# Retention values of a hybrid decoder block in one 512-column unit behind attention

## The chip, the cores and the metric

The kernel runs on one core of a Trainium2 chip. The metric is device time in microseconds (us) of one launch; smaller is better. A core has five engines that work side by side and hand tiles to one another: TensorE (PE, matrix products), VectorE (DVE), ScalarE (ACT), GpSimd (POOL) and SyncE (SP, which here only starts transfers).

## The reference

One decoder block over 512 tokens of width 1024. Two branches stand side by side, a retention branch (4 heads, key width 128, value width 256) and a block-sparse attention (8 heads of 64). Each goes through an output projection, sigmoid gates mix them, and a SwiGLU block of hidden width 2816 follows.

```python
def reference(x, norm1_w, w_in, q_norm_w, k_norm_w, w_ret_out, w_moba_out, w_o,
              norm2_w, w_ffn_gate, w_ffn_up, w_ffn_down):
...
        h = rmsnorm(x, norm1_w[l])
        proj = h @ w_in[l]
        rq, rk, rv, rg, mq, mk, mv, ga, gb = jnp.split(proj, split_points, axis=-1)

        rq = rotary(rq.reshape(B, S, RET_HEADS, RET_DK), pos)
        rk = rotary(rk.reshape(B, S, RET_HEADS, RET_DK), pos) * (RET_DK ** -0.5)
        rv = rv.reshape(B, S, RET_HEADS, RET_DV)
        ret = jax.nn.silu(rg) * retention(rq, rk, rv)
        a = ret @ w_ret_out[l]
...
        b = moba_attention(mq, mk, mv) @ w_moba_out[l]

        mix = jax.nn.sigmoid(ga) * a + jax.nn.sigmoid(gb) * b
        x = x + mix @ w_o[l]

        h2 = rmsnorm(x, norm2_w[l])
        f = (jax.nn.silu(h2 @ w_ffn_gate[l]) * (h2 @ w_ffn_up[l])) @ w_ffn_down[l]
        x = x + f
```

Inside `retention`, for each head: scores of queries with keys times a decay mask, times the values, then a normalisation of each token over the head's 256 columns (mean and variance). The values `rv` are 1024 columns of the projection, 256 for each head. This change is about how they are computed and when.

## The kernel before

**Tiling.** A tile is 128 partitions by up to 512 columns of float32 (a full PSUM bank) or 1024 columns (SBUF). Each float32 operand is split in a high part, rounded to the format of TensorE (`fp32r`), and a low part, the rest; `mm3` (L470) makes one product out of three matmuls: high by high, high by low, low by high. The high part is a cast by ScalarE (L418 for weights: `wh<-raw`), the low part a subtraction by VectorE (`wl<-raw,wh`). VectorE and TensorE record through one helper, so their lines all read L222.

**Units.** The projections run as units of Strassen-Winograd: the inner width 1024 and the columns are halved, and seven products (B11, T1, T2, B21, B22, T3, T4) stand for eight. A product is 24 matmuls (8 pieces by `mm3`), a unit 168. Some of the weight operands are sums of weight quarters, made by the transfer itself (GpSimd's accumulating queue) or by VectorE (`raw<-raw,raw`). Results of the products are combined by ScalarE copies and VectorE adds when they leave PSUM. A unit of kind W has the weights stationary and 256 tokens moving; one of kind X has the activations stationary and the weights moving, 256 columns at a time (class `Quarters`) or 512 (class `WideQuarters`, two banks for each product).

**Order.** `ORDER` (L45) lists the units of the first half of the kernel: `rk` queries and keys of two retention heads, `rv` values of two heads (kind X, 256 columns), `rg` the retention gate, `ga` and `gb` the mixing gates, `b` and `a` the output projections of attention and of retention. `NORMAL` (L80) is the order of products in a unit; in it the bank of B21 is seeded by a ScalarE copy of B11's result, and `/` puts T4 off into the next unit. The weights follow the same plan: `load_w` starts the transfer of a weight tile as soon as an earlier one's buffer is free, `more_raws` adds or takes buffers.

**Work beside.** After every group of matmuls the kernel calls `advance` (which takes a step of the queue `later`: splits, rotary steps, copies out of PSUM) and `run_bg`, which takes one entry of the list `bg`: attention first, then retention. For each pair of heads, `rv_out` (L1265) splits the values and then queues `ret_scores` (L1293), `ret_values` (L1319), the gates and, after the last pair, `ret_finish` (L1378): statistics, `ret_norm`, and `ret_transpose`, which turns the normalised rows into `ret`, the moving operand of unit `a`. Everything runs in the order in which it is written on each engine; what stands between two engines is a semaphore wait.

**Ends.** In the SwiGLU block `Hidden.c11` (L1672) adds and applies Silu. `last` (L1757) writes the last rows out: one half copied by ScalarE and sent from its queue, the other copied by VectorE and sent from SyncE's.

Of the kernel before, what the change touches and what calls it, by code (L numbers as in the profile page):

```python
# [13 lines left out]
ALU = mybir.AluOpType  # L14
# [27 lines left out]
WIDE = 4  # L42
OEXTRA = 5
FEXTRA = -2
ORDER = (("rk", 0), ("rv", 0), ("gb", 0), ("rk", 1), ("rv", 1), ("rg", 1), ("gb", 1), ("b", 0), ("b", 1), ("ga", 0), ("a", 0), ("ga", 1), ("a", 1))  # L45
# [14 lines left out]
NLAG = 2  # L60
OAHEAD = (6, 10)
# [21 lines left out]
DOWN = "B11 B21 T1 T2 B22 T3 / T4"  # L83
ALONE = "B11 B21 T1 T2 B22 T3 T4z"


def weight_plan():
# [31 lines left out]
    for name, i in ORDER:  # L119
        if name == "rg":  # L120
            cols(C_RG + 512 * i)
        elif name == "rv":
            cols(C_RV + 512 * i)
        elif name == "rk":
            wino("w_in", C_RQ + 256 * i, "w_in", C_RK + 256 * i)
        elif name == "a":
            feat(sum([group("w_ret_out", (4 * i + ct) * P, KT) for ct in range(4)], []))
        elif name == "b":
            feat(sum([group("w_moba_out", (4 * i + ct) * P, 4) for ct in range(4)], []))
        else:  # L130
            c = {"ga": C_GA, "gb": C_GB}[name] + 512 * i
            wino("w_in", c + 256, "w_in", c)
# [37 lines left out]
def hybrid_block(ctx: ExitStack, tc: tile.TileContext, wall, xin, xtok, n2, cin, out):  # L170
# [652 lines left out]
    def wino_unit(w, ev, hooks={}):  # L823
# [22 lines left out]
        seed = order[1] != "B21"  # L846
# [79 lines left out]
    class WideQuarters:  # L926


        def __init__(self, out):
            self.out = out  # L930
            self.tiles = big(nm("qa")), big(nm("qb"))
            self.a, self.b = ((t[:, :512], t[:, 512:]) for t in self.tiles)

        def p1(self, x, i, z):
            A.copy(z[i], x[i])
# [7 lines left out]
        def c11(self, z, i):  # L943
            self.out(0, 0, i, z[i])
# [278 lines left out]
    def rot_out(h0):  # L1223
        def f(r, c, x):
# [32 lines left out]
            later(d + 4, lambda: V.tensor_tensor(part["L"], two(a), part["H"].bitcast(F32), ALU.subtract))  # L1257
        return f
# [6 lines left out]
    def rv_out(h0):  # L1265
        def f(pair, i, x):
            rv[h0 + i, pair] = split(f"rv{h0 + i}_{pair}", x, None, 0 if i == 0 else SLAG[1])
            if (pair, i) == (1, 0):
                a, b = ([lambda h=h, j=j: ret_scores(h, j) for j in range(NT)] for h in (h0, h0 + 1))
                v, w = ([lambda h=h, p=p: ret_values(h, p) for p in range(2)] for h in (h0, h0 + 1))  # L1270
                fs = gates(h0 // 2)
                bg.extend(a + fs[:3] + v + b + [fs[3], None, None] + w + [None])
                ret_done("rv")
        return f
# [17 lines left out]
    def ret_scores(h, j):  # L1292
# [15 lines left out]
        def first():  # L1308
            V.scalar_tensor_tensor(tmp, ps[:, d0:d0 + P], s, tri, ALU.mult, ALU.mult)
            if rest:  # L1310
                A.activation(H[:, o], ps[:, d0 + P:w], AF.Copy, scale=s)

# [9 lines left out]
    def ret_values(h, pair):  # L1322
        ps = side_ps()
        for i in (2 * pair, 2 * pair + 1):
            c = (i % 2) * 256
            for j in range(i + 1):
# [3 lines left out]
                    rv[h, j // 2][:, (j % 2) * 256:(j % 2) * 256 + 256], j == 0, j == i)  # L1330
        def stats():
            for i in (0, 1):
# [3 lines left out]
            if pair == 0:  # L1336
                ro[h, 0], ro[h, 1] = halves(f"ro{h}")
            A.copy(ro[h, pair], ps)
# [53 lines left out]

    def rv_unit(n):
        wino_unit(hW, Quarters(rv_out(2 * n)))
# [77 lines left out]
    def branch(cts, n, mov, evac):  # L1472
# [5 lines left out]
        "rg": rg_unit, "rk": rk_unit, "rv": rv_unit,  # L1478
# [9 lines left out]
    for name, n in ORDER:  # L1488
        make[name](n)
    assert not bg  # L1490
# [163 lines left out]
    class Hidden:  # L1654
# [17 lines left out]
        def c11(self, z):  # L1672
            if not self.whole:
                V.tensor_tensor(self.a0, z, self.a0, ALU.add)
                z = self.a0
# [79 lines left out]
    def last(banks, i):  # L1755
# [7 lines left out]
        for c, copy, queue in ((slice(0, 256), A.copy, nc.scalar), (slice(256, 512), V.tensor_copy, nc.sync)):  # L1763
            y = act(nm("y"))[:, :256]
            copy(y, banks[i][:, c])
# [89 lines left out]
```

## Time and profile before

| | us |
|---|---|
| median of 3 runs | 778.69 |
| lowest and highest of them | 778.56, 778.98 |
| the profiled execution, own time | 778.98 |
| span of its profile | 777.2 |

The span is the time from the first to the last record of the trace; the execution's own time has 1.8 us more around it. The profile gives the busy time of each engine, the chain of work that ended last, and for each instruction its start, its duration and what the engine waited for ahead of it. On TensorE, matmuls are pipelined: one lasts longer than the distance from its start to the next one's, so the pace is read from starts.

### The profile page before, as it was taken

The numbers are of one execution on the slowest core, as the hardware profiler recorded it, in microseconds if no ns is written. First come the engines' busy times: TensorE is split into PE (matmuls) and PEld (weight loads), VectorE is DVE, ScalarE is ACT, GpSimd is POOL, SyncE is SP. The second block draws the span as 40 slices with busy tenths as digits, with TensorE's granted clock in tenths as the row PEclk, the third lists the DMA queues.
The fourth block names the chain that finished last, engine by engine and source line by source line (L and its number), as shares of the span: only waits on it lengthen the run. The fifth ranks groups of instructions, "written<-read, shape, count | busy, mean of one in ns | idle before, by whom it ended". The sixth has DMA issues, their size and how long they took to land.

```text
span 777.2 us, 13314 instructions
## 1 busy us (share of the span) xinstructions
PE 770.4 (99%) x5224; PEld 702.1 (90%) x5224; DVE 630.8 (81%) x959; ACT 454.3 (58%) x746; POOL 68.7 (9%) x83
## 2 busy tenths in 40 slices
PE   9999999999999999999999999999999999999997
PEld 6888888889999998989988899989999899988996
DVE  7988688887797677758588998899787977789786
ACT  8656587876675485734355775655554455655451
POOL 0001000000101000000001000111001110110000
PEclk9999999999999999999999999999999999999999
DMA  9947542536768474554898714789556993779502
GB/s 327 356 121 191 129 83 65 140 102 158 190 169 203 115 216 112 163 136 132 256 330 243 177 36 115 195 196 292 159 149 153 266 263 103 171 209 288 119 2 109
DMA packets 40959, 134.85 MB, mean 174 GB/s; under 512 B 4544, under 2 KB 5568, under 8 KB 40896
## 3 DMA queue, kind: packets, MB, share of 16 engines
q1 hardware_dynamic: 29088, 94.41, 34.3%
q0 software_dynamic: 11376, 39.06, 28.5%
q8 instruction: 41, 0.67, 0.4%
q10 hardware_dynamic: 432, 0.52, 0.2%
q14 instruction: 22, 0.18, 0.1%
HBM read 131.88 MB, written 2.10 MB: 172 GB/s over the span
## 4 chain that ended last, share of the span: by engine, by line
PE 86%; DVE 5%; issue 3%; ACT 3%; DMA 2%; POOL 0%; SPq 0%; ACTq 0%; DVEq 0%; POOLq 0%
PE pm L222 78%; PE ps L222 8%; DMA raw<-wall 2%; DVE wl L222 1%; DVE h L222 1%; DVE ws L222 1%; ACT wh L418 1%; DVE mx L222 1%; ACT f L1594 0%; ACT p L1115 0%; DVE qb L222 0%; DVE rot L222 0%; POOL raw L345 0%; ACT h L1582 0%; DVE gsl L222 0%
## 5 line engine op out<-in xcount | busy, mean ns | idle before, releaser
L222 DVE TENSOR_TENSOR wl<-raw,wh 128x1024 fp32r<-128x1024 f32 x209 | 252.5, 1220 | 48.7 <-ACT wh L418 41.6
L418 ACT CAST wh<-raw 128x1024 fp32r<-128x1024 f32 (+1 forms) x230 | 225.6, 1008 | 65.6 <-DVE raw L222 38.0
L222 PE MATMUL pm<-h,wh 128*128 128x256 f32 x1248 | 225.2, 283 | 0.2 <-ACT fa L1667 0.2
L222 PEld LDWEIGHTS pm<-h,wh 128*128 128x128 f32 x1248 | 195.1, 192 | 0.9 <-ACT fa L1667 0.4
L222 PE MATMUL pm<-h,wl 128*128 128x256 f32 x624 | 176.6, 283 | 0.0
L222 PEld LDWEIGHTS pm<-h,wl 128*128 128x128 f32 x624 | 119.7, 192 | 0.0
L345 POOL DMA_DIRECT2D raw<-wall x60 | 54.0, 900 | 455.3 <-DMA raw<-wall 230.7
L222 PE MATMUL pm<-hS,wh 128*128 128x256 f32 x384 | 71.4, 285 | 0.0
L222 PE MATMUL pm<-wh,hA 128*128 128x256 f32 (+1 forms) x256 | 66.4, 336 | 0.0
L222 PEld LDWEIGHTS pm<-hS,wh 128*128 128x128 f32 x384 | 59.9, 191 | 0.3 <-issue 0.2
L222 PE MATMUL pm<-wh,hS 128*128 128x256 f32 (+1 forms) x256 | 57.2, 311 | 0.0
L222 PE MATMUL pm<-hS,wl 128*128 128x256 f32 x192 | 54.3, 283 | 0.0
L222 PE MATMUL pm<-hA,wh 128*128 128x256 f32 x288 | 53.5, 285 | 0.0
L222 DVE TENSOR_TENSOR raw<-raw,raw 128x1024 f32<-128x1024 f32 (+1 forms) x41 | 48.2, 1181 | 0.4
L222 PEld LDWEIGHTS pm<-wh,hA 128*128 128x128 f32 x256 | 44.4, 190 | 4.2
L222 PEld LDWEIGHTS pm<-hA,wh 128*128 128x128 f32 x288 | 45.2, 191 | 1.1 <-issue 0.3
L222 PEld LDWEIGHTS pm<-wh,hS 128*128 128x128 f32 x256 | 42.8, 190 | 2.8 <-issue 0.2
L222 PE MATMUL pm<-wl,hA 128*128 128x256 f32 (+1 forms) x128 | 42.2, 330 | 0.0
L222 PE MATMUL pm<-hA,wl 128*128 128x256 f32 x144 | 40.7, 283 | 0.0
L222 PE MATMUL pm<-wh,gsh 128*128 128x512 f32 x112 | 39.8, 390 | 0.0
L222 PE MATMUL pm<-wl,hS 128*128 128x256 f32 (+1 forms) x128 | 39.6, 309 | 0.0
L222 PE MATMUL pm<-ret,wh 128*128 128x512 f32 x128 | 39.5, 390 | 0.0
(257 smaller groups left out, 1377.7 us busy)
## 6 DMA issues: line engine op xcount, KB each, us to landing
raw<-wall SPq DMA_DIRECT2D x155, 512.0 KB, 5.3
raw<-wall POOLq DMA_DIRECT2D x70, 512.0 KB, 7.0
raw<-wall SPq DMA_DIRECT2D x21, 256.0 KB, 4.6
raw<-wall POOLq DMA_DIRECT2D x9, 256.0 KB, 7.3
xr<-xtok SPq DMA_DIRECT2D x4, 512.0 KB, 5.8
x<-xin SPq DMA_DIRECT2D x7, 256.0 KB, 5.3
out<-xr SPq DMA_DIRECT2D x7, 256.0 KB, 2.1
cs<-cin SPq DMA_DIRECT2D x1, 512.0 KB, 5.5
```

The lines of the kernel that those rows point to most:

```text
L222: return f(out, *args, **kw)
L345: nc.gpsimd.dma_start(t[:, s], wall[c, :, s], accum_op=ALU.add)
L418: A.copy(h, src)
```

## The change

The two units `rv` of 256 columns become one unit `rvv` of 512 columns, placed where attention ends. Its product order `EARLIER` does not seed the bank of B21: ScalarE copies B11's result to SBUF, and VectorE adds it after B21. The splits of the second column half (heads 2 and 3) are put off by `VLAG` = 20 steps; the scores of head 0 are queued beside the unit after `RGAP` = 8 steps; two more weight buffers are open during the unit. The retention work of heads 2 and 3 is queued after the last rotary step of `rk` 1. `rg` stands ahead of `rk` 1, and both `ga` units ahead of the `a` units. In `ret_values` and `ret_scores` the ScalarE instruction that reads a bank now comes ahead of VectorE's. In the SwiGLU block one Silu is put off by two steps. At the end ScalarE makes both copies, and the queues change places.

```diff
@@ weight plan and constants
+WIDE2 = 2
+VLAG = 20
-ORDER = (("rk", 0), ("rv", 0), ("gb", 0), ("rk", 1), ("rv", 1), ("rg", 1), ("gb", 1), ("b", 0), ("b", 1), ("ga", 0), ("a", 0), ("ga", 1), ("a", 1))
+ORDER = (("rk", 0), ("gb", 0), ("rvv", 0), ("rg", 1), ("rk", 1), ("gb", 1), ("b", 0), ("b", 1), ("ga", 0), ("ga", 1), ("a", 0), ("a", 1))
+RGAP = 8
+SILU = 2
+EARLIER = "B11 *1 B21 T1 T2 B22 T3 / T4"
+        elif name == "rvv":
+            units.append(("X", ("w_in", halves, (C_RV, C_RV + 512), 512), EARLIER))
-        seed = order[1] != "B21"
+        seed = [q for q in order if q[0] not in "*/"][1] != "B21"
@@ class WideQuarters
-        def p1(self, x, i, z):
-            A.copy(z[i], x[i])
+        def p1(self, x, i, z=None):
+            if z:
+                A.copy(z[i], x[i])
+                return
+            if i == 0:
+                self.first[0], self.first[1] = halves(nm("qc"))
+            A.copy(self.first[i], x[i])
         def c11(self, z, i):
-            self.out(0, 0, i, z[i])
+            if not self.first:
+                self.out(0, 0, i, z[i])
+                return
+            f = self.first.pop(i)
+            V.tensor_tensor(f, f, z[i], ALU.add)
+            later(1, lambda: self.out(0, 0, i, f))
@@ rot_out
+            if (r, c, h0) == (1, 0, 2):
+                later(d + 5, lambda: ret_heads(2))
@@ values of retention
-    def rv_out(h0):
-        def f(pair, i, x):
-            rv[h0 + i, pair] = split(f"rv{h0 + i}_{pair}", x, None, 0 if i == 0 else SLAG[1])
-            if (pair, i) == (1, 0):
-                a, b = ([lambda h=h, j=j: ret_scores(h, j) for j in range(NT)] for h in (h0, h0 + 1))
-                v, w = ([lambda h=h, p=p: ret_values(h, p) for p in range(2)] for h in (h0, h0 + 1))
-                fs = gates(h0 // 2)
-                bg.extend(a + fs[:3] + v + b + [fs[3], None, None] + w + [None])
+    def rv_unit():
+
+        def out(r, c, i, x):
+            t = 2 * r + i
+            later(VLAG if c else 0, lambda: keep(c, t, x))
+            if (r, c, i) == (1, 0, 1):
                 ret_done("rv")
-        return f
+                ret_heads(0)
+
+        def keep(c, t, x):
+            y = split(f"rv{c}_{t}", x, None, SLAG[1])
+            for h in (0, 1):
+                rv[2 * c + h, t] = y, h * 256
+
+        wino_unit(hW, WideQuarters(out))
+
+    def ret_heads(h0):
+
+        a, b = ([lambda h=h, j=j: ret_scores(h, j) for j in range(NT)] for h in (h0, h0 + 1))
+        v, w = ([lambda h=h, p=p: ret_values(h, p) for p in range(2)] for h in (h0, h0 + 1))
+        fs = gates(h0 // 2)
+        if h0:
+            bg.extend(a + fs[:3] + v + b + fs[:3] + w)
+            ret_done("rv")
+        else:
+            bg.extend(fs[:3] + v + b + [fs[3], None, None] + w + [None])
@@ ret_scores
         def first():
-            V.scalar_tensor_tensor(tmp, ps[:, d0:d0 + P], s, tri, ALU.mult, ALU.mult)
             if rest:
                 A.activation(H[:, o], ps[:, d0 + P:w], AF.Copy, scale=s)
+            V.scalar_tensor_tensor(tmp, ps[:, d0:d0 + P], s, tri, ALU.mult, ALU.mult)
@@ ret_values
         def stats():
+            if pair == 0:
+                ro[h, 0], ro[h, 1] = halves(f"ro{h}")
+            A.copy(ro[h, pair], ps)
             for i in (0, 1):
                 bs = tp.tile([P, 6], F32, name=nm("bs"), tag="bs", bufs=4)
                 V.bn_stats(bs, ps[:, i * 256:(i + 1) * 256])
                 V.bn_aggr(mvs[:, h * NT + 2 * pair + i, :], bs)
-            if pair == 0:
-                ro[h, 0], ro[h, 1] = halves(f"ro{h}")
-            A.copy(ro[h, pair], ps)
@@ main loop
     for name, n in ORDER:
+        if name == "rvv":
+            more_raws(WIDE2)
+            bg.extend([None] * RGAP + [lambda j=j: ret_scores(0, j) for j in range(NT)])
         make[name](n)
+        if name == "rvv":
+            more_raws(-WIDE2)
@@ Hidden.c11
                 V.tensor_tensor(self.a0, z, self.a0, ALU.add)
-                z = self.a0
+                later(SILU, lambda: A.activation(self.a0, self.a0, AF.Silu))
+                return
@@ last
-        for c, copy, queue in ((slice(0, 256), A.copy, nc.scalar), (slice(256, 512), V.tensor_copy, nc.sync)):
+        for c, queue in ((slice(0, 256), nc.sync), (slice(256, 512), nc.scalar)):
             y = act(nm("y"))[:, :256]
-            copy(y, banks[i][:, c])
+            A.copy(y, banks[i][:, c])
             queue.dma_start(out[:, 3, c], y)
```

How the rows stand on the engines is shown at three places. A row is one instruction (`x2`: two alike in a row) with its output, its inputs and its shape; the number behind a tile's name only tells buffers apart.

On TensorE, at the start of the second `rv` unit before; `hA` is the stationary activation, `wh` and `wl` the high and low part of the moving weights:

```order
L222 MATMUL pm_2684<-wh_2519,hA_128 128x256
L222 MATMUL pm_2684<-wl_2543,hA_128 128x256
L222 MATMUL pm_2684<-wh_2519,hA_128 128x256 x2
L222 MATMUL pm_2684<-wl_2543,hA_128 128x256
L222 MATMUL pm_2684<-wh_2519,hA_128 128x256
L222 MATMUL pm_2684<-wh_2519,hA_156 128x256
L222 MATMUL pm_2684<-wl_2543,hA_156 128x256
```

On TensorE in the new unit, in its product T1 (`hS` is a sum of activations); `pm_2148` and `pm_2149` are the two banks of a product:

```order
L229 MATMUL pm_2148<-wh_2085,hS_418 128x512
L229 MATMUL pm_2148<-wl_2102,hS_418 128x512
L229 MATMUL pm_2148<-wh_2085,hS_418 128x512 x2
L229 MATMUL pm_2148<-wl_2102,hS_418 128x512
L229 MATMUL pm_2148<-wh_2085,hS_418 128x512
L229 MATMUL pm_2149<-wh_2085,hS_418 128x512
L229 MATMUL pm_2149<-wl_2102,hS_418 128x512
```

Where a piece of the old unit writes 256 columns with each matmul, one of the new unit writes 512; the unit has as many matmuls as each of the old two, so 336 of 256 columns go and 168 of 512 come.

On VectorE before, from the first rotary step on the output of T4 of `rk` 1 (`rot<-pm,cs`) to the low part of those queries or keys (the last `rL`); `wl` are weights of the units around, `rv` is a value split:

```order
L222 TENSOR_TENSOR rot_2807<-pm_2301,cs 128x512
L222 TENSOR_TENSOR rL_2_2749<-rot_2717,rH_2_2748 128x2x256
L222 TENSOR_TENSOR wl_2840<-raw_2545,wh_2824 128x1024
L222 TENSOR_TENSOR rot_2807<-rot_2807,cs 128x512
L222 TENSOR_TENSOR rot_2807<-rot_2807 128x512
L222 TENSOR_TENSOR wl_2874<-raw_2634,wh_2857 128x1024
L222 TENSOR_TENSOR rv_0_2872<-pm_236,rv_0_2872 128x512
L222 TENSOR_TENSOR wl_2895<-raw_2771,wh_2879 128x1024
L222 TENSOR_TENSOR rL_2_2671<-rot_2807,rH_2_2670 128x2x256
L222 TENSOR_TENSOR qb_2683<-qb_2683,pm_2721 128x512
```

On VectorE after, from the same step to the same result and to the low part of the first weight of `b` 0 (`wl_3192`):

```order
L229 TENSOR_TENSOR rot_3092<-pm_2662,cs 128x512
L229 TENSOR_TENSOR rL_2_3035<-rot_3003,rH_2_3034 128x2x256
L229 TENSOR_TENSOR wl_3125<-raw_2883,wh_3109 128x1024
L229 TENSOR_TENSOR rot_3092<-rot_3092,cs 128x512
L229 TENSOR_TENSOR rot_3092<-rot_3092 128x512
L229 TENSOR_TENSOR qa_2968<-pm_236,r1b 128x512
L229 TENSOR_TENSOR wl_3158<-raw_2748,wh_3142 128x1024
L229 TENSOR_TENSOR rL_2_2964<-rot_3092,rH_2_2963 128x2x256
L229 TENSOR_TENSOR qb_2969<-qb_2969,pm_3007 128x512
L229 TENSOR_TENSOR wl_3192<-raw_2949,wh_3176 128x1024
```

In the place of two weight parts and a value split, one gate product (`qa`) and one weight part stand ahead of the last `rL`; and behind it, on TensorE, the scores of head 2 and then unit `b` 0 follow five products after the start of T4, where before eight and a half products lay between the start of T4 and those scores.

On TensorE before, at the last of the transposes that make `ret` (`ps<-cst,ro`), which stand in a unit `ga`; the first matmul of `a` that reads `ret` comes 40 rows further on:

```order
L222 MATMUL pm_236<-hA_210,wh_3783 128x256 x2
L222 MATMUL pm_236<-hA_210,wl_3806 128x256
L222 MATMUL ps_3939<-cst,ro_3468 128x128 x4
L222 MATMUL ps_3944<-cst,ro_3468 128x128 x4
L222 MATMUL pm_236<-hA_183,wh_3783 128x256 x2
L222 MATMUL pm_236<-hA_183,wl_3806 128x256
```

On TensorE after, in the first block of `a` 0 (`pm<-ret,wh`):

```order
L229 MATMUL pm_4072<-ret_4005,wh_4020 128x512 x2
L229 MATMUL pm_4072<-ret_4005,wl_4037 128x512
L229 MATMUL ps_4092<-cst,ro_3646 128x128 x4
L229 MATMUL ps_4097<-cst,ro_3646 128x128 x4
L229 MATMUL pm_4072<-ret_4051,wh_4020 128x512 x2
L229 MATMUL pm_4072<-ret_4051,wl_4037 128x512
L229 MATMUL pm_4072<-ret_4053,wh_4020 128x512 x2
L229 MATMUL pm_4072<-ret_4053,wl_4037 128x512
L229 MATMUL pm_4072<-ret_4102,wh_4020 128x512 x2
L229 MATMUL pm_4072<-ret_4102,wl_4037 128x512
```

The last eight transposes now stand in the block that reads them: six matmuls with earlier tiles lie between them and the first matmul that needs their result, and its second one needs the low part.

## Rows read from the trace of the kernel before

**Rows 1.** The page, busy time (share) and count by engine; then TensorE's granted clock

```profile
PE 770.4 (99%) x5224; PEld 702.1 (90%) x5224; DVE 630.8 (81%) x959; ACT 454.3 (58%) x746; POOL 68.7 (9%) x83
...
PEclk9999999999999999999999999999999999999999
```

**Rows 2.** The page, shares of the chain that ended last

```profile
PE 86%; DVE 5%; issue 3%; ACT 3%; DMA 2%; POOL 0%; SPq 0%; ACTq 0%; DVEq 0%; POOLq 0%
```

**Rows 3.** Waits of TensorE, whole span: total us, times, longest

```profile
PE ps L549 <- DVE warm L222: 1.2, 1, 1.2
PE ps L222 <- ACT p L1115: 0.4, 1, 0.4
PE ps L222 <- ACT pt L1152: 0.3, 1, 0.3
PE pm L222 <- ACT pm L1538: 0.2, 1, 0.2
PE pm L222 <- ACT fa L1667: 0.2, 1, 0.2
PE pm L222 <- DVE mh L222: 0.2, 1, 0.2
```

**Rows 4.** The chain, 214 to 248 us: start, length, what

```profile
215.33 31.68 PE pm L222 x264
```

**Rows 5.** Timeline of TensorE, a unit with 512 columns: start, length, instruction, count

```profile
59.66 0.62 PE L222 MATMUL pm<-wh,hS 128*128 128x512 f32 x2
...
61.70 0.62 PE L222 MATMUL pm<-wh,hS 128*128 128x512 f32 x2
```

**Rows 6.** Timeline of TensorE, T4 of `rk` 1 and the next product's start

```profile
222.37 0.40 PE L222 MATMUL pm<-hA,wh 128*128 128x256 f32 x2
...
225.25 0.28 PE L222 MATMUL pm<-wh,hS 128*128 128x256 f32 x1
```

**Rows 7.** Timeline of VectorE, the steps up to the last `rL`

```profile
233.00 1.22 DVE L222 TENSOR_TENSOR wl<-raw,wh 128x1024 fp32r<-128x1024 f32 x1
234.13 0.69 DVE L222 TENSOR_TENSOR rv<-pm,rv 128x512 fp32r<-128x512 f32 x1
234.74 1.22 DVE L222 TENSOR_TENSOR wl<-raw,wh 128x1024 fp32r<-128x1024 f32 x1
235.87 0.69 DVE L222 TENSOR_TENSOR rL<-rot,rH 128x512 fp32r<-128x512 f32 x1
```

**Rows 8.** Busy time by engine, one stretch: us, then PE, PEld, DVE, ACT, POOL

```profile
215.00:247.00 32.00, 32.00 (x268) 32.00 (x268) 29.27 (x39) 22.43 (x32) 4.31 (x5) 1.00 0.72 180
```

**Rows 9.** Timelines of TensorE, ScalarE and VectorE at the last transposes

```profile
325.61 1.04 PE L222 MATMUL ps<-cst,ro 128*128 128x128 f32 x8
326.40 0.48 PE L222 MATMUL pm<-hA,wh 128*128 128x256 f32 x2
...
326.24 1.07 ACT L489 CAST ret<-ps 128x512 fp32r<-128x512 f32 x2 [1.22 <-PE ps L222]
...
326.86 1.29 DVE L222 TENSOR_TENSOR ret<-ps,ret 128x512 fp32r<-128x512 f32 x2 [1.08 <-ACT ret L489]
```

**Rows 10.** The page's groups: busy, mean ns, idle before and its releaser

```profile
L222 DVE TENSOR_TENSOR wl<-raw,wh 128x1024 fp32r<-128x1024 f32 x209 | 252.5, 1220 | 48.7 <-ACT wh L418 41.6
```

**Rows 11.** Groups of ScalarE, the copy of a values bank

```profile
L1338 ACT COPY ro<-ps 128x512 f32<-128x512 f32 x8 | 4.7, 586 | 13.6 <-DVE bs L222 13.4
```

**Rows 12.** Timelines of ScalarE and VectorE, the statistics of retention

```profile
286.94 1.28 ACT L511 ACT_TABLE_LOAD   x1
...
289.20 0.18 DVE L222 TENSOR_TENSOR gn_t<-gn_t,gnv 128x16 f32<-128x16 f32 x1
```

**Rows 13.** Timeline at the end, ScalarE, VectorE and SyncE

```profile
772.83 0.37 ACT L1765 COPY y<-pm 128x256 f32<-128x256 f32 x1 [0.77 <-PE pm L222]
...
773.23 0.42 DVE L222 COPY y<-pm 128x256 f32<-128x256 f32 x1 [1.24 <-ACT y L1765]
773.68 0.33 SPq L1766 DMA_DIRECT2D out<-y  x1
```

More of the change, by code (lines that the diff above doesn't have):

```diff
@@ L929, in __init__ @@
         def __init__(self, out):
-            self.out = out
+            self.out, self.first = out, {}
             self.tiles = big(nm("qa")), big(nm("qb"))
             self.a, self.b = ((t[:, :512], t[:, 512:]) for t in self.tiles)
-        def p1(self, x, i, z):
-            A.copy(z[i], x[i])
+        def p1(self, x, i, z=None):
[5 more added lines that the diff above has]
+            A.copy(self.first[i], x[i])
         def p5(self, y, i):
@@ L1329, in ret_values @@
                 mm3(ps[:, c:c + 256], tuple(x[:, o:o + P] for x in sc[h, key]),
-                    rv[h, j // 2][:, (j % 2) * 256:(j % 2) * 256 + 256], j == 0, j == i)
+                    rv[h, j][0][:, rv[h, j][1]:rv[h, j][1] + 256], j == 0, j == i)
         def stats():
+            if pair == 0:
+                ro[h, 0], ro[h, 1] = halves(f"ro{h}")
+            A.copy(ro[h, pair], ps)
             for i in (0, 1):
@@ L1391, in rk_unit @@
         wino_unit(hW, Quarters(rot_out(2 * n)))
-    def rv_unit(n):
-        wino_unit(hW, Quarters(rv_out(2 * n)))
     sga, sgb, mixT = {}, {}, {}
@@ L1477, in hybrid_block @@
     make = {
-        "rg": rg_unit, "rk": rk_unit, "rv": rv_unit,
+        "rg": rg_unit, "rk": rk_unit, "rvv": lambda n: rv_unit(),
         "ga": lambda n: gate_unit(sga, 4 * n),
```

## The prediction

> **What bounds the kernel now.** I read the page's busy times first. TensorE is busy for 770.4 of the 777.2 us of the span, and its granted clock stands at nine tenths or more, the top digit, in every slice [rows 1]. The chain of work that ended last says the same: 86% TensorE, with 5% VectorE the next [rows 2]. A busy engine may still hide small stalls, so the list of TensorE's waits comes next: 1.2 us ahead of its first matmuls, and five waits of 0.2 to 0.4 us, 1.3 us together, in all the rest [rows 3]. So the time is the sum of the paces of TensorE's matmuls. A change pays if it shortens that sum, and costs if it makes TensorE wait for something that today is ready just in time. VectorE is the engine nearest to that: in the stretch from 215 to 247 us it is busy for 29.27 of 32.00 us while TensorE is busy for all 32.00 [rows 8]. So a VectorE load of 91% alone makes nobody wait.
>
> The pace has to be read from starts, since matmuls overlap. With 256 columns, 264 matmuls in a row took 31.68 us, 120.0 ns each [rows 4]. With 512 columns, the rows at 59.66 and 61.70 us are nine matmuls apart (three products by `mm3`), 2.04 us or 226.7 ns each [rows 5]. Two of 256 thus cost 240.0 ns, one of 512 does 226.7: twice the columns at 13.3 ns less.
>
> **The change part by part.** *The wide unit.* It removes 336 matmuls of 256 columns (40.32 us) and brings 168 of 512 (38.09 us): 168 × 13.3 ns = **2.23 us less**, all of it on the engine that sets the end. The count of weight casts, low parts and transfers is the same on both sides; only their places move with the units.
>
> The Trainium skill, page "TensorE: Matmul & The Clock Gate", section "Back-to-back issue gap", gives an isolated matmul N/2.4 ns plus 2.5 ns; by that, joining two would save 2.5 ns, and the unit 0.42 us, an estimate from that page. The page calls this the gap of isolated matmuls, and the two paces of [rows 4, 5] don't agree with it.
>
> *What comes on other engines.* Without the seeded bank VectorE has two more additions of 128x512, at about 0.6 us from start to start (234.13 to 234.74) [rows 7]: 1.2 us on an engine that TensorE doesn't wait for there. ScalarE's copy goes to another place at the same size. I take 0; without cover it is 1.2 us.
>
> *ScalarE reads first.* Today ScalarE's eight copies of a values bank stand idle for 13.4 us behind VectorE's statistics, though a copy lasts 0.59 us [rows 11]. Turned round, VectorE may wait up to 0.59 us for each copy, 4.7 us in all, spread over many places, and ScalarE's casts behind come earlier. TensorE waits for neither in today's list [rows 3]. I take 0; a wait of 0.6 us at one tight place is the bound.
>
> *The scores of heads 2 and 3, now just behind `rk` 1.* Today T4 of `rk` 1 starts at 222.37 us and a product lasts 2.88 us (to 225.25) [rows 6]; the last `rL` ends at 235.87 + 0.69 = 236.56 [rows 7], 14.19 us after that start. In the new order five products (14.40 us) lie between that start and the scores, and their second matmul, which reads `rL`, comes at 14.63. If VectorE runs as today up to 233.00, the new order puts `qa` there (0.6), then one low part (1.13 from start to start), then `rL`, done at 235.42: 13.05 after T4's start, 1.6 us early. Next come `qb` and the low part for `b` 0: 235.33 and 235.93, done at 237.15, or 14.78; needed by the third matmul of `b` 0, at 14.40 + 5 × 0.227 = 15.53. So 0.75 us is left. VectorE later by one low part (1.13) costs 0.4 us, by two 1.5. I take 0.1.
>
> *The last transposes, now inside `a` 0.* Today the eight start at 325.61, the next matmul at 326.40, and the first low part of the pair is done at 326.86 + 0.69 = 327.55, 1.94 us after the start [rows 9]. In the new order the reader of that low part comes 0.79 + 7 × 0.227 = 2.38 us after the start, so 0.44 us is left; today the first reader stands 40 rows further on. One low part of weights late costs 0.7 us, two cost 1.8. VectorE's load there, from the end of the statistics to `ret`'s last low part: nine low parts and two sums of weights at 1.22 us, 27 operations of 512 columns at 0.69, nine tiny ones at 0.18 [rows 7, 12], 33.7 us. TensorE meanwhile has 228 matmuls of 256 columns, 24 of 512 and 32 transposes (0.79/8 each), 36.0 us. That is 94%, against 91% in the stretch without a wait [rows 8]. I take 0.1.
>
> *The rest.* Attention now stands beside `rk` 0, `gb` 0 and the wide unit's start; its waits of 0.4 and 0.3 us [rows 3] may go or double: 0. The Silu put off by two steps can at most take away the wait of 0.2 us for ScalarE's first activation of such a unit, or add one like it: 0. Two more weight buffers let transfers start earlier, none later: 0.
>
> *The end.* Today ScalarE copies from 772.83 for 0.37 us, VectorE starts at 773.23, when that is over, lasts 0.42, and SyncE sends at 773.68 [rows 13]. With both on ScalarE the second ends at about 773.2 + 0.37 = 773.57 and is sent from its own queue: 0.1 us less, between 0 and 0.2.
>
> **Sum**: −2.23 − 0.1 + 0.2 = −2.13 us. The profiled execution itself took 778.98 us, 1.8 more than its span, and lies 0.3 above the median; the same difference on the median of 778.69 gives 776.56, so **776.6 us**. With no new wait it is 776.4, and 775.1 if today's 1.3 us of small waits go too.
>
> **The rivals.** *The gain is partly given back at the two tight places.* VectorE arrives one or two low parts late at `b` 0 and at `a` 0: 0.4 + 0.7 = 1.1 us to 1.5 + 1.8 = 3.3 us, so 776.4 + 1.1 = 777.5 to 779.7, most likely near 778.0. For it speaks that both margins (0.75 and 0.44 us) are shorter than one low part; against it that VectorE lives with 91% today without any wait of TensorE [rows 8].
>
> *VectorE and ScalarE become the bound between the statistics and `a` 0, and the kernel gets slower.* The load of 33.7 us holds no waiting. Today each low part has 48.7/209 = 0.23 us idle ahead of it, most of it for ScalarE's cast [rows 10], and each pair of `ret` low parts 1.08 us [rows 9]. If all that came on top, 9 × 0.23 + 4 × 1.08 = 6.4 us, and a table load of 1.28 us ahead of the square root [rows 12], VectorE would need 41.4 us where TensorE has 36.0: 5.4 late, and 776.4 + 5.4 = **781.8 us**. It decides for slower from 3.9 us late. Against it: the idle time of an engine that is ahead of its work vanishes when it falls behind, and the four pairs lie between other work.
>
> *The wider matmul doesn't pay as read.* The pace of 512 was read where weights and activations of the first unit move; beside the scores and attention the new unit might run at 227 + 13 = 240 ns, no gain: 778.69 − 0.1 + 0.2 = 778.8. Against it, the pace of 256 is the same 120.0 ns through all of [rows 4], with side work near it. A fixed cost per matmul well below the 13.3 ns is the milder form of this case.
>
> By the Trainium skill's formula above, 2.5 ns a matmul, the time would be 778.4 us; the two paces read here leave it no more than a small part of this case's chance.
>
> **How the numbers follow.** About 0.2%, 1.56 us, is what a measurement of this kernel can tell from no change: faster is below 777.1, slower above 780.2. The forecast (775.1 to 777.1) gets 0.64; waits at the tight places 0.25, of which the lowest part is at the edge of faster; the slower rival 0.07; a wide matmul that doesn't pay 0.04. So faster 0.65, within 0.2% 0.27, slower 0.08. The range: from 775.6, more than half of today's small waits gone, to 778.8, which takes in the greater part of the second case and the last; outside are the slower rival, the worst of the second case, and a little below.
>
> **What would show it.** Right: TensorE's busy time and the distance of its first and last matmul fall by about 2.2 us; rows of the new unit stand 0.68 us apart for three matmuls; the waits of TensorE stay a handful of 0.2 to 0.4 us. Wrong: a wait of TensorE for VectorE's `rL`, or `wl` at the start of `b` 0; a wait for `ret` in `a` 0's first block; idle time of TensorE in `ga` 1; or three matmuls of the new unit at 0.72 us. The last copy at the end should stand on ScalarE, directly behind the first.

## The result: slower, where faster was forecast

The median of four executions is **785.63 us** (783.72 to 787.96), that of before in the same comparison 778.84. The ratio is 1.0091 with an interval of 1.0079 to 1.0103: 0.9% slower, where 776.6 us was forecast with 778.8 as the upper end. The profiled execution took 783.72 us with a span of 781.7 us, 4.5 more than before.

The page of after (busy us, share and count of each engine) shows the matmuls that were to go:

```profile
PE 770.1 (99%) x5056; PEld 693.4 (89%) x5056; DVE 630.0 (81%) x960; ACT 456.3 (58%) x747; POOL 68.7 (9%) x83
```

TensorE has 168 instructions fewer and VectorE one more [rows 1]. In the new unit, TensorE's timeline (start, length, instruction, count) has the pace that was forecast:

```profile
186.27 0.62 PE L229 MATMUL pm<-wh,hS 128*128 128x512 f32 x2
...
188.31 0.62 PE L229 MATMUL pm<-wh,hS 128*128 128x512 f32 x2
```

Nine matmuls take 2.04 us, 226.7 ns each, as in [rows 5]. The gain of 2.23 us is there, and so 4.5 + 2.2 = 6.7 us were lost elsewhere. TensorE's waits (total us, times, longest; four smaller or unchanged kinds left out) name most of it:

```profile
PE pm L229 <- ACT pm L909: 1.8, 1, 1.8
PE pm L229 <- DVE qb L229: 1.5, 1, 1.5
PE ps L556 <- DVE warm L229: 1.2, 1, 1.2
PE pm L229 <- DVE wl L229: 0.8, 2, 0.5
PE ps L229 <- DVE rL L229: 0.5, 1, 0.5
...
PE pm L229 <- ACT pt L1169: 0.4, 1, 0.4
```

Against [rows 3] five kinds of some size are new: `pm` for ScalarE's copy `pm<-pm` (L909), then `qb`, `wl` and `rL` of VectorE, and a small one for attention's `pt`. All waits listed, small ones included, are 7.3 us together, 2.5 before; that is 4.8 of the 6.7 us. The other 1.9 lie in time that counts as busy, which is why TensorE's busy time fell by 0.3 us and not by the 2.2 that the prediction named as its first sign. TensorE's timeline shows where (what it waited for stands at the end):

```profile
262.08 0.28 PE L229 MATMUL pm<-hS,wl 128*128 128x256 f32 x1
263.87 0.48 PE L229 MATMUL pm<-hA,wh 128*128 128x256 f32 x2 [1.51 <-DVE qb L229]
...
275.71 0.50 PE L229 MATMUL pm<-hS,wh 128*128 128x256 f32 x2
276.48 0.39 PE L229 MATMUL pm<-hS,wl 128*128 128x256 f32 x1 [0.27 <-DVE wl L229]
...
279.20 0.39 PE L229 MATMUL ps<-rH,rH 128*128 128x512 f32 x1
280.14 0.50 PE L229 MATMUL ps<-rL,rH 128*128 128x512 f32 x1 [0.55 <-DVE rL L229]
...
280.70 0.63 PE L229 MATMUL pm<-moT,wh 128*128 128x512 f32 x2
281.87 0.50 PE L229 MATMUL pm<-moT,wl 128*128 128x512 f32 x1 [0.54 <-DVE wl L229]
...
318.66 0.28 PE L229 MATMUL pm<-hS,wl 128*128 128x256 f32 x1
320.74 0.50 PE L229 MATMUL pm<-hS,wh 128*128 128x256 f32 x2 [1.80 <-ACT pm L909]
```

Read by starts, against paces of 0.120 and 0.227 us, the loss is 1.67 at 263.87 (T4 of `rk` 1), 0.53 at 276.48, 0.71 at 280.14 (scores of head 2), 0.72 at 281.87 (first weights of `b` 0) and 1.96 at 320.74 (product T2 in `ga` 0): 5.6 of the 6.7 us. The remaining 1.1 us is in small pieces, beside attention for the most part. T4 waits there because it adds to the bank that VectorE's `qb` has still to read; 276.48 is in T3 of `gb` 1. The chain of waits (start, length, what) leads from the late scores and `b` 0 back to one weight tile, the second of `gb` 1:

```profile
242.47 5.27 DMA raw<-wall
247.78 0.47 issue
248.27 6.99 DMA raw<-wall
255.36 1.05 ACT wh L425
```

Its first transfer starts at 242.47, the accumulating one lands at 255.3, and the cast follows at once; VectorE stood idle for 4.36 us until that cast was done, and what is written behind it came later with it:

```profile
256.44 1.23 DVE L229 TENSOR_TENSOR wl<-raw,wh 128x1024 fp32r<-128x1024 f32 x1 [4.36 <-ACT wh L425]
...
279.40 0.69 DVE L229 TENSOR_TENSOR rL<-rot,rH 128x512 fp32r<-128x512 f32 x1
```

The last `rL` stands 15.53 us after the start of T4 (279.40 − 263.87), where before it was 13.50 [rows 6, 7] and the prediction had 12.36.

### The profile page after: what moved, and what is told of

The parts are those of the page before. It is cut to its first block, busy times and chain, and to the rows that moved or that the text cites. A ratio compares the mean times of both kernels' runs of the same rounds, so it can differ in the third digit from the quotient of the medians.

```text
span 781.7 us, 12991 instructions
## 1 busy us (share of the span) xinstructions
PE 770.1 (99%) x5056; PEld 693.4 (89%) x5056; DVE 630.0 (81%) x960; ACT 456.3 (58%) x747; POOL 68.7 (9%) x83
## 4 chain that ended last, share of the span: by engine, by line
PE 88%; DVE 5%; ACT 3%; DMA 2%; issue 1%; SPq 0%; ACTq 0%; POOLq 0%; DVEq 0%
PE pm L229 81%; PE ps L229 7%; DMA raw<-wall 2%; DVE wl L229 1%; DVE rot L229 1%; ACT wh L425 1%; DVE mx L229 1%; ACT p L1132 0%; DVE rL L229 0%; DVE qb L229 0%; ACT rot L1249 0%; DVE qa L229 0%; ACT rot L1250 0%; ACT rH L1263 0%; DVE p L229 0%
## 5 line engine op out<-in xcount | busy, mean ns | idle before, releaser
L229 PE MATMUL pm<-wh,hA 128*128 128x512 f32 (+1 forms) x208 | 64.2, 375 | 0.4 <-ACT pt L1169 0.4
L229 PE MATMUL pm<-wh,hS 128*128 128x512 f32 (+1 forms) x192 | 53.1, 354 | 0.0
L229 PEld LDWEIGHTS pm<-wh,hA 128*128 128x128 f32 x208 | 37.8, 189 | 7.1 <-ACT pt L1169 0.6
L229 PEld LDWEIGHTS pm<-wh,hS 128*128 128x128 f32 x192 | 34.4, 189 | 5.0
L229 PE MATMUL pm<-wl,hA 128*128 128x512 f32 (+1 forms) x104 | 38.1, 366 | 0.0
L229 PEld LDWEIGHTS pm<-hS,wl 128*128 128x128 f32 x192 | 36.7, 191 | 0.5 <-DVE wl L229 0.5
```

The lines of the kernel that those rows point to most:

```text
L229: return f(out, *args, **kw)
```

## The experiments

Each is compared with the kernel before at about 778.6 us; a "wait" is one of TensorE unless another engine is named. "After" is the changed kernel (785.63 us, span 781.7). All start from the changed kernel unless another is named.

### Transfers, order and buffers

**The additional weight buffers stay open until `rk` 1 is over.**

```diff
-        if name == "rvv":
+        if (name, n) == ("rk", 1):
             more_raws(-WIDE2)
```

> The changed kernel, but the two extra weight buffers are given back after unit rk 1 instead of right after the wide unit, so that the weight transfers behind the wide unit start two buffers earlier. Late-transfer theory: the waits of TensorE at 264 (1.7 us), 276 (0.7) and 280 to 282 us (1.4) come from one weight tile that lands at 255 us and holds ScalarE for 6.2 us and VectorE for 4.4; they go, the span falls by 3 to 4 us to about 778, and the wait of 2.0 us at 321 stays. Load theory: VectorE is behind there by its own work and the new order; less than 1 us of these waits goes, span 781 or more.

Measured: 789.21 us, ratio 1.0132 [1.0116, 1.0148], where the late-transfer theory expected 3 to 4 us less than after. ScalarE's wait for a transfer is gone, but more waits take its place. Between 200 and 300 us, VectorE and ScalarE now wait for TensorE to give SBUF tiles back (the rows of this kernel, then of after, then of before):

```profile
DVE wl L229 <- PE pm L229: 12.2, 6, 3.1
ACT wh L425 <- PE pm L229: 9.6, 9, 1.9
```

```profile
DVE wl L229 <- PE pm L229: 6.2, 3, 3.0
ACT wh L425 <- PE pm L229: 7.3, 5, 1.9
ACT wh L425 <- DMA raw<-wall: 6.2, 1, 6.2
```

```profile
DVE wl L222 <- PE pm L222: 2.9, 1, 2.9
ACT wh L418 <- PE pm L222: 1.1, 2, 0.8
ACT wh L418 <- DMA raw<-wall: 4.3, 2, 2.3
```

Weights, their high and low parts, rotary results and gate products all come from one ring of 47 tiles (`PAIRS`). Earlier transfers only take tiles that casts and low parts then lack. A part of this kernel's time is clock (see the last section), which a sum of waits doesn't hold.

**One more weight buffer closed behind the unit**, against the pressure on the ring.

```diff
-            more_raws(-WIDE2)
+            more_raws(-WIDE2 - 1)
```

> The changed kernel with one raw weight buffer fewer after the wide unit. Buffer theory: all 1024-column tiles share 47 SBUF buffers; from 250 to 290 us the live ones fill the ring, so high and low parts of weights wait until TensorE gives a buffer back, and run no longer ahead of it. One raw tile fewer leaves a buffer to the split weights: the waits from 264 to 282 us (3.5 us) fall by 1 to 3 us, span about 779 to 781. Transfer theory: fewer raw tiles start their transfers later, the waits grow, span 783 or more.

Measured: 794.89 us, 1.0204 [1.0162, 1.0246]: 9 us more than after, where 1 to 3 less were expected if a tile is worth more to the split weights than to a transfer. A wait of 3.2 us for a cast comes at 265, and three waits of 5.2 us together come in the SwiGLU block (by the program the buffer stays closed to the end).

**The ring one tile smaller**, in the changed kernel and in the one before.

```diff
-PAIRS = 47
+PAIRS = 46
```

> The changed kernel with 46 instead of 47 shared SBUF buffers, nothing else. Buffer theory: the waits between 220 and 300 us grow by 1 to 4 us, and ScalarE's casts and VectorE's low parts wait for TensorE for more than the 9.6 and 15.4 us of the changed kernel. If buffers aren't short, the span stays within 0.5 us of 781.7.

> The kernel before with 46 instead of 47 shared SBUF buffers, nothing else. Buffer theory: before has a buffer to spare nearly everywhere (its split weights are 2 to 14 us ahead of TensorE), so it loses little: 0 to 0.5 us, time 778.7 to 779.2. If one buffer fewer costs before 2 us or more too, the changed kernel's loss is not a matter of what it holds in addition.

Measured: 795.05 us (1.0201 [1.0179, 1.0223]) in the changed kernel, 9.4 us more (7.8 in span, 789.5 to 781.7, with the granted clock of both profiled executions at 0.999); 779.67 (1.0011 [1.0001, 1.002]) in the one before, 0.9 us more by the ratio, with one wait added (1 to 4 us and 0 to 0.5 had been expected):

```profile
PE pm L222 <- DVE qb L222: 0.7, 1, 0.7
```

So one tile is worth some ten times as much after the change as before it: the changed kernel is short of SBUF tiles. In the kernel before, the lost tile also shows as a late transfer: between 200 and 300 us ScalarE's casts wait for transfers for 6.4 us (longest 5.4) in place of 4.3 (longest 2.3). In the changed kernel that wait falls to 3.8 us, and the loss stands in other waits, between 233 and 328 us.

**No delay of the value splits of heads 2 and 3.** The four splits turn two waiting tiles into four.

```diff
-VLAG = 20
+VLAG = 0
```

> The changed kernel without the delay of the splits of heads 2 and 3 (0 instead of 20 steps). Buffer theory: the delay keeps the four values tiles in two buffers for longer; without it two more are held from 190 to 230 us, where the ring is full, and the waits grow there: span 783 to 786. Load theory: it only moves four casts and four low parts to an earlier place, where VectorE has room: span the same or 1 us less.

Measured: 790.08 us, 1.0139 [1.0116, 1.0163]. Earlier splits cost 4.4 us more, as a shortage of tiles would have it; 783 to 786 had been expected. They also bring work of ScalarE and VectorE forward, which this run doesn't separate, and a part is clock, as in the first of these experiments.

**`rk` 1 ahead of `rg` 1**, so that the scores of heads 2 and 3 are no longer just behind `rk` 1.

```diff
-("rvv", 0), ("rg", 1), ("rk", 1), ("gb", 1),
+("rvv", 0), ("rk", 1), ("rg", 1), ("gb", 1),
```

> The changed kernel with unit rk 1 ahead of rg 1, as before, so that a whole unit lies between the last rotary step and the scores of heads 2 and 3. Adjacency theory: the waits at the scores and at the first weights of b 0 (0.7 us each) go, and with them part of those ahead: span about 779 to 780. Late-transfer theory: the tile that is late stays late; a wait of 1 to 2 us for VectorE stays in this stretch, span 781 or so.

Measured: 792.02 us, 1.0163 [1.014, 1.0186]. The wait at these scores is gone, but waits for VectorE and ScalarE of 1.6 to 2.9 us come elsewhere. The order that sets the two apart is thus no cure; 779 to 780 had been expected if their standing next to each other were the cause.

### ScalarE's queue at `ga` 0

ScalarE's timeline of after shows why T2 of `ga` 0 waits until 320.74:

```profile
316.56 0.46 ACT L1345 ACTIVATE sc<-ps,sk 128x256 fp32r<-128x256 f32 x1
318.11 0.30 ACT L1349 CAST sc<-dia 128x128 fp32r<-128x128 f32 x1 [1.09 <-DVE dia L229]
318.32 0.36 ACT L1345 ACTIVATE sc<-ps,sk 128x128 fp32r<-128x128 f32 x1
318.58 1.04 ACT L425 CAST wh<-raw 128x1024 fp32r<-128x1024 f32 x1
319.90 0.30 ACT L1349 CAST sc<-dia 128x128 fp32r<-128x128 f32 x1 [0.28 <-DVE dia L229]
320.10 0.58 ACT L909 COPY pm<-pm 128x512 f32<-128x512 f32 x1
```

T2 adds to the bank that holds B11's result, so it can't start before the copy that carries this result into B21's bank (L909, the seed copy) has read it. T1's matmuls follow B11's from 315.90 and are over at 318.9, but the copy is queued behind scores of head 3, which wait for VectorE.

**The seed copy written ahead of them.**

```diff
+    seed_now = [False]
...
+                now = seed_now[0] and (q, j, i) == ("B11", len(ws) - 1, 1)
+                if now:
+                    out(bank)
...
-                elif j == len(ws) - 1 and i == 1:
+                elif j == len(ws) - 1 and i == 1 and not now:
                     later(1, lambda: out(bank))
...
+        seed_now[0] = (name, n) == ("ga", 0)
         make[name](n)
+        seed_now[0] = False
```

> The changed kernel, but in unit ga 0 the ScalarE copy of B11's result, for which TensorE waits 2.0 us at 321 us, is written ahead of the score casts of head 3 that stand in front of it. If the wait comes from ScalarE's place in line (casts that wait for VectorE's diagonal products), it falls below 0.3 us: span about 779.9. If VectorE is what is late, another wait of 1 to 2 us takes its place right behind: span 781 to 782.

Measured: 782.36 us, 1.0049 [1.0033, 1.0065]; the span is 779.7, 2.0 less, as the wait was; the other large waits stay. This mends 2.0 of the 6.7 us of span.

**VectorE reads the retention banks first, as before.**

```diff
         def first():
+            V.scalar_tensor_tensor(tmp, ps[:, d0:d0 + P], s, tri, ALU.mult, ALU.mult)
             if rest:
                 A.activation(H[:, o], ps[:, d0 + P:w], AF.Copy, scale=s)
-            V.scalar_tensor_tensor(tmp, ps[:, d0:d0 + P], s, tri, ALU.mult, ALU.mult)
@@ stats
-            A.copy(ro[h, pair], ps)
             for i in (0, 1):
...
+            A.copy(ro[h, pair], ps)
```

> The changed kernel, with VectorE reading the score and value banks first again, as before. If ScalarE-first holds VectorE back (it stands idle 11.4 us for ScalarE ahead of the diagonal products and 7.9 us ahead of the statistics), the wait of 2.0 us at 321 us goes and the span falls by about 2 us to 780. If it only changes who waits for whom, the span stays within 1 us of 781.7, or rises because ScalarE's casts come later.

Measured: 788.65 us, 1.0123 [1.0107, 1.0139], so with ScalarE first the changed kernel is better off. The wait for the seed copy is longer here, and the granted clock falls at its end (stretch; its length, busy us of PE, PEld, DVE, ACT and POOL, granted clock, share and GB/s of transfers):

```profile
PE pm L229 <- ACT pm L909: 3.2, 1, 3.2
```

```profile
320.00:325.00 5.00, 2.08 (x9) 2.08 (x10) 4.16 (x10) 3.65 (x7) 0.86 (x1) 0.70 1.07 221
325.00:330.00 5.00, 5.00 (x29) 5.00 (x29) 0.52 (x2) 1.64 (x2) 0.00 (x0) 0.62 0.45 138
```

The wait grew by 1.4 us, the span by 5.1 (786.8). The means of these stretches take in full speed at their ends: in stretches of 1 us the clock is at 0.50 or 0.51 from 322 to 328 us and at 0.58 in the next, so from the end of the wait at 322.9 TensorE ran about 5.9 us at half speed. That costs some 3 us, an estimate from these rows. The other waits of TensorE are 1.0 us longer together (6.5 for 5.5), and the three make up the 5.1 within the estimate.

### The unit at other places

Three orders put the wide unit ahead of `gb` 0, all with the seed copy mended, with `rk` 1 ahead of `rg` 1 and with `ga` and `a` in turn as before: the second brings `rk` 1 forward too, the third puts `gb` 0 behind `rg` 1. So each moves several units at once.

```diff
-ORDER = (("rk", 0), ("gb", 0), ("rvv", 0), ("rg", 1), ("rk", 1), ("gb", 1), ("b", 0), ("b", 1), ("ga", 0), ("ga", 1), ("a", 0), ("a", 1))
+ORDER = (("rk", 0), ("rvv", 0), ("gb", 0), ("rk", 1), ("rg", 1), ("gb", 1), ("b", 0), ("b", 1), ("ga", 0), ("a", 0), ("ga", 1), ("a", 1))
...
+ORDER = (("rk", 0), ("rvv", 0), ("rk", 1), ("gb", 0), ("rg", 1), ("gb", 1), ("b", 0), ("b", 1), ("ga", 0), ("a", 0), ("ga", 1), ("a", 1))
...
+ORDER = (("rk", 0), ("rvv", 0), ("rk", 1), ("rg", 1), ("gb", 0), ("gb", 1), ("b", 0), ("b", 1), ("ga", 0), ("a", 0), ("ga", 1), ("a", 1))
```

> The wide unit in the place of the old first rv unit, beside attention, ahead of gb 0; rk 1 ahead of rg 1, and ga and a units alternating, as before; the early copy in ga 0 kept. So the width without the place behind attention. If the loss comes from retention of heads 2 and 3 being done late, with queries, keys and values held in buffers until 300 us, it is smaller here only where their tiles are given back sooner; by the count of live tiles the ring is still full from 240 to 290 us: TensorE's waits 2 to 5 us, span 777 to 780. If the place alone is at fault, no waits, span 775.0.

> As the kernel with the wide unit early, but rk 1 directly behind the wide unit and gb 0 after it, so that retention of heads 2 and 3 starts three units sooner and gives its tiles back by 270 us. By the count of live tiles the ring is less full after 250 us (40 to 43 of 47 against 44 to 47). Buffer theory: waits of TensorE after 250 us vanish; what is left is between 160 and 240 us. Span 775 to 778, time 777 to 780. If it is above 782 the buffers of the later stretch were not the cause.

> As the one before, with gb 0 moved behind rg 1, so that its four gate tiles are filled one unit later. Buffer theory: 2 to 4 more buffers are free from 230 to 260 us, and the waits there are smaller than in the kernel with rk 1 early; span 775 to 777. If the load of VectorE at rk 1 beside the scores sets them, they are the same or larger.

Measured: 792.34 us (1.0185 [1.0154, 1.0215]), 792.93 (1.0181 [1.0165, 1.0196]) and 789.11 (1.0135 [1.0119, 1.015]). All three have new waits beside attention (`pt` 1.4 and `qc` 1.4 us), where unit and attention now share VectorE, and keep others at 220 to 305 us. None comes near the 782.36 us of the same seed copy at the place of the change. Spans of 775 to 780 us were expected, for the last two because a count of live tiles found the ring less full, and 789.6, 789.1 and 786.3 were measured; for the second a time above 782 had been named as a sign that the buffers of the later stretch are not the cause. Casts and low parts do wait less for TensorE here (between 200 and 300 us 9.5, 4.1 and 6.8 us, 13.5 in after, summed over the two rows shown above), and the kernels are slower all the same. So these runs speak against tiles as the only cause, and that count of tiles did not predict a time.

### Is the late transfer a cause or a consequence?

Both start from the kernel with the seed copy mended (782.36 us). One puts the splits off further, which frees tiles and leaves the number of weight buffers; the other opens no additional buffers.

```diff
-VLAG = 20
+VLAG = 40
```

> The changed kernel with the seed copy of ga 0 written ahead of the score casts (782.36 us), and the value splits of heads 2 and 3 put off by 40 steps in place of 20. Buffer theory: each split makes two SBUF tiles out of one that waits, so later splits free buffers while the wide unit and rg 1 run; the waits of TensorE at 263 to 282 us (1.63 + 0.42 + 0.71 + 0.71 = 3.5 us) shrink by at least one us and the time comes to 779 to 781.5. Late-transfer theory: the transfers are as they were, the wait at 263 us stays at 1.6, and the time at 782 to 783. A new wait of attention's successors for the splits themselves would show as a wait for an rv tile.

```diff
-WIDE2 = 2
+WIDE2 = 0
```

> The changed kernel with the seed copy of ga 0 written ahead of the score casts (782.36 us), and no additional weight buffers during the wide unit. Late-transfer theory: it is the closing of the two buffers behind the unit that holds the weights of gb 1 back; without opening and closing, ScalarE's wait of 6.2 us for a transfer is gone, the wait of TensorE at 263 us too, and the time is about 780.5. Buffer theory: the ring of SBUF tiles is as full as before, casts and low parts wait for TensorE by 10 us and more, and the time is 782 to 784. If two fewer buffers starve the wide unit itself, a wait for a weight part comes at 195 to 225 us.

Measured: 781.52 us (1.0036 [1.0023, 1.0049]) and 784.72 (1.0084 [1.0067, 1.0101]): the first at the upper edge of what the buffer theory expected, the second just above it. With later splits the transfer itself comes earlier. From 228 to 243 us, SyncE, which has to issue it, waits for TensorE to give a buffer back, first in after, then here:

```profile
SPq L350 <- PE pm L229: 7.4, 1, 7.4
```

```profile
SPq L350 <- PE pm L229: 4.0, 1, 4.0
```

ScalarE's wait for the transfer (200 to 300 us) falls from 6.2 to

```profile
ACT wh L425 <- DMA raw<-wall: 1.2, 1, 1.2
```

and the wait of 1.5 us for `qb` at T4 of `rk` 1 is gone from TensorE's list, which now has

```profile
PE pm L229 <- DVE wl L229: 1.2, 2, 0.6
PE pm L229 <- DVE mh L229: 1.0, 1, 1.0
PE pm L229 <- ACT pm L1581: 0.7, 1, 0.7
...
PE ps L229 <- DVE rL L229: 0.3, 1, 0.3
```

Without the additional buffers, casts wait 9.5 us for transfers and the `qb` wait is still 0.9: closing them was not the cause. **So the transfer is late because of when tiles are taken and given back, not because the two buffers are closed.** That it is the full ring is argued from this and from the kernels with 46 tiles: casts and low parts wait for TensorE no less with the later splits (8.2 and 8.2 us, 7.3 and 6.2 in after), so what the splits give up goes to the transfer. What the later splits do not cure are the scores and `b` 0 (`rL`, `wl`): the four splits, 0.6 us of VectorE each, now lie there. The gain in span is nil here, since the seed copy's kernel has none of two waits found here, `mh` at 7 us, ahead of all that the edit touches, and L1581 at 436 us, in the output projection; the median is 0.8 us lower, within the spread of the two.

### The small edits in the kernel before

ScalarE first, the Silu put off and both last copies on ScalarE with the queues changed, without the wide unit; then the Silu alone, and ScalarE first alone.

```diff
@@ ret_scores
-            V.scalar_tensor_tensor(tmp, ps[:, d0:d0 + P], s, tri, ALU.mult, ALU.mult)
             if rest:
                 A.activation(H[:, o], ps[:, d0 + P:w], AF.Copy, scale=s)
+            V.scalar_tensor_tensor(tmp, ps[:, d0:d0 + P], s, tri, ALU.mult, ALU.mult)
@@ ret_values
+            A.copy(ro[h, pair], ps)
             for i in (0, 1):
...
-            A.copy(ro[h, pair], ps)
@@ Hidden.c11
-                z = self.a0
+                later(SILU, lambda: A.activation(self.a0, self.a0, AF.Silu))
+                return
@@ last
...
-            copy(y, banks[i][:, c])
+            A.copy(y, banks[i][:, c])
```

> The kernel before with the small edits alone: ScalarE reads retention banks first, one Silu of the SwiGLU units two steps later, both last copies on ScalarE. The prediction gave these -0.1 us (end) and 0: span 777.1, time 778.6. If the Silu delay removes TensorE's wait for ScalarE in the SwiGLU part, 0.2 to 0.9 us less, 777.7 to 778.4. If ScalarE-first costs VectorE time where it is tight, up to 2 us more.

> The kernel before, with nothing but the Silu put off by two steps. If the waits of TensorE in the SwiGLU block (0.2 us for ScalarE's first activation there, 0.1 beside it) are what it takes away: 778.2 to 778.5. If the gain of 1.0 us of the three small edits together comes mostly from the copies that read retention banks first, 778.6 to 778.8, no difference.

> The kernel before, with nothing but ScalarE's reading of the retention banks (scores and values) put ahead of VectorE's. The prediction gave it 0. If it carries the gain of the three small edits together (1.0 us): 777.8 to 778.2. If the Silu and the end carry it: 778.5 to 778.9.

Measured: **777.66 us** (0.9984 [0.9974, 0.9993]) for all, 778.0 (0.9995 [0.9985, 1.0004]) for the Silu, 778.26 (0.9997 [0.9988, 1.0007]) for ScalarE first. Together they win 1.0 us and make the fastest kernel of this study, ahead of both given ones. Alone, 0.5 and 0.2 us can't be told from nothing; the end was not run alone. The waits of the kernel with all, beside the first:

```profile
PE ps L223 <- ACT p L1116: 0.4, 1, 0.4
PE pm L223 <- DVE mh L223: 0.4, 1, 0.4
PE ps L223 <- ACT pt L1153: 0.3, 1, 0.3
PE pm L223 <- DVE ml L223: 0.2, 1, 0.2
```

Those for ScalarE in [rows 3] at L1538 and L1667 are gone.

## Why the prediction was wrong

**Right: the gain.** 336 matmuls of 256 columns gave way to 168 of 512 at 226.7 ns. The rival of a wide matmul that doesn't pay falls.

**The step that failed: "Two more weight buffers let transfers start earlier, none later: 0".** A transfer came later: one weight tile of `gb` 1 landed at 255.3 us, ScalarE had stood idle for it for 6.2 us and VectorE for 4.36, where before no wait of ScalarE for a transfer in that stretch was longer than 2.3. The two buffers themselves are not the reason, since without them TensorE still waits 0.9 us for `qb`. The step put at nothing, without a reason, what moving the unit does to the tiles. Buffers for weights come from the ring that also holds high and low parts, rotary results and gate products; with the unit moved, heads 2 and 3 come late, so their operands hold tiles for longer (this is read from the order of the program; no trace counts tiles). The prediction counted transfers and instructions, not tiles. That the kernel with 46 tiles loses 9.4 us, the one before 0.9, shows the shortage. With later splits the transfer came earlier and the wait at T4 of `rk` 1 (1.67 us) was gone, which shows that path. That the full ring made the transfer late is the likeliest reading, not shown by itself.

SyncE's wait of 7.4 us for TensorE is no sign of it: in the kernel before SyncE waits as long for TensorE (25.0 us in five waits between 205 and 262 us, the longest 8.9; after 24.2 in five, the longest 7.4).

**The condition "if VectorE runs as today up to 233.00" failed with it.** From `rot` to the last `rL` VectorE did what was forecast (5.80 us, 5.92 forecast), but it came there late: `rL` started 15.53 us after T4 in place of 12.36, which used up the margin of 1.6 us at the scores; the 0.75 us at `b` 0 went too. The rival of the two tight places had the waits at the scores and at `b` 0 (0.71 and 0.72 us) and a place at `a` 0, which held: no wait for `ret` is in the list. The rival sized VectorE's lateness at one or two low parts (1.1 or 2.3 us), the runs show 3.2 us.

**Not in the prediction: the seed copy in `ga` 0**, 1.96 us. The `ga` units were moved next to the scores of head 3, and a copy that TensorE waits for came to stand behind casts that wait for VectorE. The prediction looked at VectorE's queue there, not at ScalarE's. Written ahead of them, the copy gave back 2.0 us of span and 3.3 of the median, of which a part can be clock.

**The end.** Both copies stand on ScalarE, as forecast, and the halves are sent from SyncE's and ScalarE's queue:

```profile
777.62 0.65 ACT L1803 COPY y<-pm 128x256 f32<-128x256 f32 x2 [0.77 <-PE pm L229]
778.02 0.33 SPq L1804 DMA_DIRECT2D out<-y  x1
778.30 0.35 ACTq L1804 DMA_DIRECT2D out<-y  x1
```

The last transfer starts 0.68 us after the first copy's start; before it was 0.85 [rows 13]: 0.17 us, where 0.1 was forecast.

**ScalarE first and the Silu** had 0 each. With the end they are worth 1.0 us in the kernel before, and in the changed kernel ScalarE first alone saves 3.0 us of the median: without it the wait for the seed copy is 1.4 us longer and the clock falls at its end. The rival that ends slower named another place (between the statistics and `a` 0), which shows no wait: its sign came true, its mechanism did not. Its load of 33.7 us was also counted high: it adds durations, while VectorE starts low parts 1.13 us apart and operations of 512 columns 0.60 [rows 7], which makes about 30 us, an estimate from these rows.

**What stays open.** With the seed copy mended and the splits later, the kernel is still 3.1 us behind before. Its waits at the scores and at `b` 0 come behind VectorE's queue, and about one us lies beside attention, where attention's neighbours changed with the order and which no run took apart. That width and place could be had without these waits by another order was not shown. A ring of 48 tiles, the direct test of the shortage from the other side, was not run.

## What to carry to other kernels

Before a unit is moved, ask how long its results hold SBUF tiles at the new place: in a ring that weights share, a result that is consumed later can take the lead away from the transfers. The plain test is one tile fewer in both kernels (9.4 and 0.9 us here). Waits in the rows are weaker signs: SyncE waits for TensorE as long in the kernel before, and casts and low parts waited less in orders that were slower. Look through the queue of each engine for what lands ahead of an instruction that TensorE waits for, ScalarE's as well as VectorE's. And run the small edits by themselves: here they carried a gain that the large one hid.

## What the hardware showed

TensorE's granted clock fell to half, the lower of its two levels (1.2 GHz for 2.4), at or just behind some of its waits and not at others, and in these runs the length of the wait alone doesn't tell which. It fell at a wait of 3.2 us in the kernel with VectorE first (rows above), and behind one of 1.9 us that ended at 243.35 in the kernel whose additional buffers stay open; it stayed full through and behind one of 3.2 us that ended at 265.36 in the kernel with one buffer fewer. The rows of the last two (the granted clock is the last number but two):

```profile
245.00:250.00 5.00, 5.00 (x33) 5.00 (x32) 1.53 (x4) 1.05 (x3) 0.86 (x1) 0.70 0.60 100
```

```profile
265.00:270.00 5.00, 4.64 (x39) 4.67 (x40) 4.00 (x7) 2.44 (x5) 0.86 (x1) 1.00 0.09 10
```

In the changed kernel, whose longest wait in the middle is 1.8 us, the clock of the profiled execution is 0.999 on the mean. Its four executions lie at 783.72 and 784.54 us with a mean clock of 0.999 and 1.000, and at 786.73 and 787.96 with 0.997 and 0.995, so that part of the median of 785.63 is clock, which the sum of waits doesn't contain; at which wait it falls in those executions no trace shows.
